# A two-block transformer kernel: both products of the squared-ReLU MLP by seven quadrant products each

## The chip, the cores and the metric

The kernel runs on one core of a Trainium2 chip. The metric is the device time of one execution in microseconds (us). Five engines work in parallel and meet at semaphores: PE (TensorE, matrix products), ACT (ScalarE), DVE (VectorE), POOL (GpSimd) and SP (SyncE, which issues the DMAs here). Each engine runs its own queue in order.

## What is computed

The program is two transformer blocks over 1024 tokens of width 1024 in float32. The first block has retention, a gated delta rule and a mixture of experts, the second neighbourhood attention, gated linear attention and an MLP. The change lies in the MLP at the end of the second block:

```
def sqrelu_mlp(h, ln_g, w1, w2):           # h 1024x1024, w1 1024x4096, w2 4096x1024
    u = rmsnorm_2(h, ln_g) @ w1
    return jnp.square(jax.nn.relu(u)) @ w2

h = h + sqrelu_mlp(h, ...)
return rmsnorm_2(h, ln_final_g)
```

## The kernel before, in words

Every float32 product is made of three matmuls in the reduced format fp32r: an operand x is split into hi (ACT copies x to fp32r, which rounds it) and lo (DVE computes x minus hi), and a product is hi·hi + hi·lo + lo·hi (`mm3`, L637; `wsplit`, L622). Each matmul takes a 128x128 weight block and streams 512 columns into one of the eight banks of PSUM.

`mlp` (L2223) first normalises the eight token tiles of `xres` and transposes them on PE into hi and lo parts that stay in SBUF (`normed_T`, `to_T`). Then a loop over 16 slices of 256 hidden channels does both products in turn. For the first, `chan_block` (L679) makes four PSUM tiles of 128 channels by 512 tokens with 24 matmuls each, and `ev_u` (L2241) applies ReLU and square and splits the result. For the second, `wload` fetches two blocks of w2, and for each of 16 tiles 6 matmuls go to PSUM, which DVE adds to `xres` (L2256). A slice has 96 + 96 = 192 matmuls, the loop 3072. Weights come from DRAM in 512 KB loads; activations and `xres` stay in SBUF throughout. At the end each token tile is normalised once more and stored (L2258 to L2265).

The order of instructions is not that of the code. `Program.record` (L325) notes every operation with its dependences, `price` (L358) gives it a cost, and `flush` (L404) plays all engines forward and emits each queue in the order so found, with the longest remaining path first. In its model POOL and DVE do not slow each other; a 1024-element `tensor_tensor` costs 1.14 us on DVE and 2.21 us on POOL, a 512-column fp32r matmul 0.213 us. Since one function emits everything, nearly all rows of the profile show line 346. SBUF is divided by hand into a float32 and an fp32r area; `Pool.tile` gives out slots in rings, and a write into a slot waits for the last readers of what was there (`alloc`, L188).

Of the kernel before, what the change touches and what calls it, by code (L numbers as in the profile page):

```python
# [12 lines left out]
F32R = mybir.dt.float32r  # L13
I32 = mybir.dt.int32
BF = mybir.dt.bfloat16
AF = mybir.ActivationFunctionType
OP = mybir.AluOpType
# [4 lines left out]
T = 1024  # L22
D = 1024
NT = 8
# [22 lines left out]
LANES = 8  # L47
TABLES = {'Exp': (0,), 'Tanh': (0, 18), 'Silu': (18,), 'Sin': (9, 18), 'Ln': (5,)}
RMW = ('copy_predicated',)


class Op:
# [102 lines left out]
class Program:  # L155
# [169 lines left out]
    def record(self, eng, name, real, a, k):  # L325
# [10 lines left out]
        for key, v in list(enumerate(args)) + list(k.items()):  # L336
            if key == 'accum_out':
                writes.append(v)
            elif key != 'out':
                if isap(v):  # L340
                    reads.append(v)
                elif isinstance(v, bass.IndirectOffsetOnAxis):
                    reads.append(v.ap)
        if name in RMW or (name == 'matmul' and not k.get('start', True)):
            reads.append(out)
# [150 lines left out]
class Cols:  # L496
# [3 lines left out]
    def add(self, name, a):  # L500
        a = np.asarray(a, np.float64)
        if a.ndim == 1:
            a = np.broadcast_to(a[None, :], (128, a.shape[0]))
        a = a.reshape(128, -1)
        self.at[name] = (self.n, a.shape[1])
        self.parts.append(a.astype(np.float32))
        self.n += a.shape[1]
# [53 lines left out]
class Kern:  # L561
# [1276 lines left out]
    def mixer2(self):  # L1838
        nc, ins = self.nc, self.ins
        w_in = ins['w_in_2'][0]  # L1840
        self.banks = {'acc': (0, 1), 'tp': (2, 3), 'sm': (4, 5), 'ga': (6, 7)}
        c0 = ExitStack()
# [6 lines left out]
        h = self.new_hT(self.pool('h2', ctx=ch))  # L1849
# [24 lines left out]
        pa = self.pa = self.pool('pa', ctx=ca)  # L1874
# [25 lines left out]
        py = self.pool('y', ctx=self.cy)  # L1900
# [4 lines left out]
        with ca:  # L1905
            self.banks.update({'sc': (0, 2), 'tp': (4, 5), 'po': (6, 7)})
            cs = ExitStack()
            self.pst = self.pool('ns', ctx=cs)
            with ExitStack() as cf:
                pf = self.pool('pf', ctx=cf)  # L1910
                slots = [[(pf if i == 3 else self.pst).get(1024, f'n{i}{j}', F32R) for i in range(4)]
                         for j in range(2)]
            order = [slots[j][i] for i in range(3) for j in range(2)]
            for n, name in enumerate(('naq', 'nakh', 'nakl')):
                self.pst.tags[name] = ([order[n], order[n + 3]], [0])
            self.P = []
            for i in range(5):
                P = self.t(pa, [128, 640], tag=f'P{i}')
                nc.gpsimd.memset(P[:, 512:640], 0.0)
                self.P.append(P)  # L1920
            self.pn = 0
            for hp in range(4):
                self.prog.boost = 0. if hp < 1 else 0.0
                st = self.na_stack(hp)
                for i in range(2):
                    self.na_head(2 * hp + i, st[i])
            self.prog.boost = 0.0
            cs.close()
            for i in range(2):
                y[i].append(self.t(py, [128, 8, 4, 128], F32R, tag=f'y{i}1'))  # L1930
            for tt in range(NT):
                ts = slice(tt * 128, tt * 128 + 128)
                g = self.t(pa, [128, 512], tag='gg', bufs=1)
                s = self.t(pa, [128, 512], tag='gs', bufs=1)
                nc.sync.dma_start(g, self.gla_d[ts])
                nc.sync.dma_start(s, self.gs_d[ts])
                nc.gpsimd.tensor_tensor(out=g, in0=g, in1=s, op=OP.mult)
                self.to_T(g, [y[0][1][:, tt]], [y[1][1][:, tt]])
        self.banks = {'acc': (0, 1, 2, 3), 'tp': (4, 5), 'sm': (6, 7)}
        self.cxp = ExitStack()  # L1940
        xp = self.pool('x2', ctx=self.cxp)
# [3 lines left out]
        for cb in range(2):  # L1945
            cs = slice(512 * cb, 512 * cb + 512)
# [3 lines left out]
            self.tok_block(ins['w_out_2'][0], 512 * cb, y, ev_o)  # L1950
        for tt in range(NT):
            self.tap('hm', self.xres[tt], slice(tt * 128, tt * 128 + 128))
        c0.close()

    def normed_T(self, pn, x, row, h, tt):
        r = self.sumsq(pn, x, 'nt')
# [263 lines left out]
                                  sr.rearrange("p h e -> p (h e)"))  # L2220


    def mlp(self):  # L2223
        nc, ins = self.nc, self.ins
        V = nc.vector
        w1, w2 = ins['w_ff1_2'][0], ins['w_ff2_2'][0]
        h = self.y
        with ExitStack() as cn:
            pn = self.pool('pn2', ctx=cn)
            row = self.bcast_row(ins['ln_ff_g_2'][0], D, 'row', pn)  # L2230
            for tt in range(NT):
                self.normed_T(pn, self.xres[tt], row, h, tt)
        for tag in ('whi', 'wlo'):
            self.wp.trim(tag, 3)
        self.nw = 3
        with ExitStack() as cu:
            pu = self.pool('pu', ctx=cu)
            for e in range(16):
                uh, ul = [self.t(pu, [128, 2, T], F32R, tag=n) for n in ('uh', 'ul')]
                for m in range(2):  # L2240
                    def ev_u(half, tok, p):  # L2241
                        t = self.t(pu, [128, 512], tag='ut', bufs=2)
                        nc.scalar.activation(t, p, AF.Relu)
                        nc.scalar.activation(uh[:, m, tok], t, AF.Square)
                        V.tensor_tensor(out=t, in0=t, in1=t, op=OP.mult)
                        V.tensor_tensor(out=ul[:, m, tok], in0=t, in1=uh[:, m, tok], op=OP.subtract)
                    self.chan_block(w1, 256 * e + 128 * m, 128, h, ev_u)
                for cb in range(2):
                    cs = slice(512 * cb, 512 * cb + 512)
                    wh, wl = self.wload(w2, 256 * e, 512 * cb, 2, 512)  # L2250
                    for tt in range(NT):
                        ts = slice(tt * 128, tt * 128 + 128)
                        p = self.ps([128, 512], 'acc')
                        for k in range(2):
                            self.mm3(p, uh[:, k, ts], ul[:, k, ts], wh[:, k], wl[:, k], k == 0, k == 1)
                        V.tensor_tensor(out=self.xres[tt][:, cs], in0=self.xres[tt][:, cs], in1=p, op=OP.add)  # L2256
        self.cy.close()
        with ExitStack() as cf:  # L2258
            pf = self.pool('pf2', ctx=cf)
            row = self.bcast_row(ins['ln_final_g_2'], D, 'row', pf)  # L2260
            for tt in range(NT):
                xt = self.xres[tt]
                r = self.sumsq(pf, xt, 'fn')
                V.scalar_tensor_tensor(xt, xt, r, row, op0=OP.mult, op1=OP.mult)
                nc.sync.dma_start(self.out[tt * 128:(tt + 1) * 128], xt)  # L2265
        self.cxp.close()
# [20 lines left out]
```

## Time and profile before

| | us |
|---|---|
| three runs | 2833.72 (median), 2832.54, 2833.97 |
| the profiled execution, its own time | 2830.14 |
| its span, first to last instruction | 2828.1 |
| first matmul of the MLP loop starts | 2114.37 |
| granted clock of TensorE, mean | 0.983 of 2.4 GHz |

The span starts with the first instruction; all positions below are us from there. A row of the timeline merges neighbouring instructions of one kind (x4 is four of them) and gives the start of the first and the time from there to the end of the last. A duration includes time in which an instruction that has been started is held up. The spacing of starts tells what one costs in a full queue.

### The profile page before, as it was taken

The numbers are of one execution on the slowest core, as the hardware profiler recorded it, in microseconds if no ns is written. First come the engines' busy times: TensorE is split into PE (matmuls) and PEld (weight loads), VectorE is DVE, ScalarE is ACT, GpSimd is POOL, SyncE is SP. The second block draws the span as 40 slices with busy tenths as digits, with TensorE's granted clock in tenths as the row PEclk, the third lists the DMA queues.
The fourth block names the chain that finished last, engine by engine and source line by source line (L and its number), as shares of the span: only waits on it lengthen the run. The fifth ranks groups of instructions, "written<-read, shape, count | busy, mean of one in ns | idle before, by whom it ended". The sixth has DMA issues, their size and how long they took to land. (4 is left out here: it accounts for less than half of the span.)

```text
span 2828.1 us, 36441 instructions
## 1 busy us (share of the span) xinstructions
PE 2663.9 (94%) x13174; PEld 2048.9 (72%) x13174; DVE 1705.0 (60%) x2575; ACT 1117.4 (40%) x1960; POOL 622.5 (22%) x675
## 2 busy tenths in 40 slices
PE   5999999999978999999986999999999999999998
PEld 4787788997757776454435777777888888888886
DVE  7557676555679888786766335277445454444445
ACT  4333223333136677565545434357422212122122
POOL 2106433432442111322136012144110000000001
PEclk9999999999979999999998999999999999999999
DMA  9443246246348999999978343263211111111111
GB/s 243 91 138 88 93 149 165 80 157 230 143 165 287 344 349 341 352 323 361 341 245 295 121 125 110 72 172 94 94 42 52 38 52 52 45 52 53 45 53 67
DMA packets 305621, 446.82 MB, mean 158 GB/s; under 512 B 61274, under 2 KB 135694, under 8 KB 304414
## 3 DMA queue, kind: packets, MB, share of 16 engines
q1 hardware_dynamic: 298782, 427.68, 46.5%
q0 software_dynamic: 6656, 16.79, 1.7%
q8 instruction: 105, 1.72, 0.2%
q14 instruction: 78, 0.64, 0.1%
HBM read 384.54 MB, written 65.75 MB: 159 GB/s over the span
## 5 line engine op out<-in xcount | busy, mean ns | idle before, releaser
L346 PE MATMUL psum_all<-sbuf 128*128 128x512 f32 (+10 forms) x13174 | 2663.9, 363 | 151.7 <-DVE sbuf L346 99.9
L346 PEld LDWEIGHTS psum_all<-sbuf 128*128 128x128 f32 (+7 forms) x13174 | 2048.9, 176 | 766.3 <-issue 167.3
L346 ACT ACTIVATE sbuf<-sbuf 128x1024 fp32r<-128x1024 f32 (+9 forms) x792 | 707.6, 914 | 781.3 <-PE psum_all L346 536.3
L346 DVE TENSOR_TENSOR sbuf<-sbuf,sbuf 128x1024 fp32r<-128x1024 f32 (+3 forms) x538 | 616.8, 1166 | 277.6 <-ACT sbuf L346 269.0
L346 ACT ACTIVATE sbuf<-psum_all 128x512 f32<-128x512 f32 (+14 forms) x798 | 377.9, 485 | 886.1 <-PE psum_all L346 839.7
L346 POOL TENSOR_TENSOR sbuf<-sbuf 128x512 f32<-128x512 f32 (+7 forms) x325 | 384.3, 1190 | 576.7 <-DVE sbuf L346 474.4
L346 DVE TENSOR_TENSOR sbuf<-sbuf,psum_all 128x512 f32<-128x512 f32 (+4 forms) x359 | 239.1, 673 | 165.2 <-PE psum_all L346 164.6
L346 DVE TENSOR_TENSOR sbuf<-sbuf 128x512 f32<-128x512 f32 (+9 forms) x285 | 205.2, 734 | 203.6 <-ACT sbuf L346 175.5
L346 POOL TENSOR_SCALAR sbuf<-sbuf 128x1 f32<-128x1 f32 (+3 forms) x182 | 75.3, 415 | 994.9 <-ACT sbuf L346 902.7
L346 DVE TENSOR_TENSOR sbuf<-psum_all,sbuf 128x512 fp32r<-128x512 f32 (+13 forms) x306 | 182.3, 607 | 158.0 <-ACT sbuf L346 78.1
L346 DVE SCALAR_TENSOR_TENSOR sbuf<-sbuf 128x512 f32<-128x512 f32 (+5 forms) x247 | 196.3, 801 | 55.6 <-POOL sbuf L346 43.1
L346 DVE TENSOR_SCALAR sbuf<-sbuf 128x32 f32<-128x32 f32 (+7 forms) x220 | 111.2, 518 | 48.1 <-ACT sbuf L346 22.7
L1728 POOL DMA_INDIRECT y_d<-sbuf x35 | 57.4, 1641 | 195.8 <-DVE sbuf L346 194.5
L346 DVE SCALAR_TENSOR_TENSOR sbuf<-psum_all,sbuf 128x128 f32<-128x128 f32 (+9 forms) x109 | 62.0, 585 | 40.0 <-PE psum_all L346 39.5
L1716 POOL DMA_INDIRECT sbuf<-h_d,sbuf x35 | 45.1, 1288 | 186.2 <-PE psum_all L346 153.2
L346 DVE SCALAR_TENSOR_TENSOR sbuf<-sbuf,psum_all 128x128 f32<-128x128 f32 (+1 forms) x100 | 38.2, 409 | 76.7 <-PE psum_all L346 51.8
L346 DVE CUSTOM_DVE_ANT_0 sbuf<-psum_all,sbuf 128x512 f32<-128x512 f32 (+2 forms) x80 | 48.1, 613 | 24.8 <-PE psum_all L346 24.2
L346 DVE COPY sbuf<-psum_all 128x512 f32<-128x512 f32 (+9 forms) x55 | 31.7, 576 | 39.9 <-PE psum_all L346 39.7
L346 POOL MEMSET sbuf<- 64x64 f32 (+10 forms) x54 | 16.8, 313 | 174.4 <-DVE sbuf L346 91.9
L346 POOL TENSOR_TENSOR sbuf<-sbuf,sbuf 128x1024 fp32r<-128x1024 f32 x16 | 40.1, 2510 | 61.7 <-ACT sbuf L346 48.4
L346 ACT ACTIVATE sbuf<-psum_all,sbuf 128x128 f32<-128x128 f32 (+1 forms) x72 | 24.4, 405 | 23.4 <-PE psum_all L346 17.7
L346 ACT ACTIVATION_READ_ACCUMULATOR sbuf<-sbuf 128x1 f32 x152 | 28.9, 190 | 0.0
(18 smaller groups left out, 111.8 us busy)
## 6 DMA issues: line engine op xcount, KB each, us to landing
sbuf<-in_w SPq DMA_DIRECT2D x384, 512.0 KB
sbuf<-in_w_ff SPq DMA_DIRECT2D x64, 512.0 KB
sbuf<-in_w_in SPq DMA_DIRECT2D x56, 512.0 KB
sbuf<-in_w_ada SPq DMA_DIRECT2D x48, 512.0 KB
sbuf<-in_x SPq DMA_DIRECT2D x16, 512.0 KB
sbuf<-in_w_out SPq DMA_DIRECT2D x16, 512.0 KB
sbuf<-y_d SPq DMA_DIRECT2D x8, 1024.0 KB
qkv_d<-sbuf SPq DMA_DIRECT2D x12, 512.0 KB
```

The lines of the kernel that those rows point to most:

```text
L346: op = self.new_op(eng, lambda: real(*a, **k), name, reads, writes)
L1716: return self.prog.real.gpsimd.indirect_dma_start(out=xg, out_offset=None, in_=self.h2_d, in_offset=bass.IndirectOffsetOnAxis(ap=tok, axis=0),
L1728: st = self.prog.real.gpsimd.indirect_dma_start(out=self.y_d, out_offset=bass.IndirectOffsetOnAxis(ap=dest, axis=0), in_=y, in_offset=None ...
```

## The change

`mlp` is rewritten. The two products (1024x1024 by 1024x4096, and 1024x4096 by 4096x1024) become eight products of 1024x1024 by 1024x1024, four for each. Each of these is cut into 512x512 quadrants and made by `wino` with seven quadrant products in place of eight (the Winograd form of Strassen's algorithm). The sums and differences of quadrants are made in place by `both`, on POOL (`G`) for six quadrants and on DVE (`V`) for two. Each quadrant product splits both its operands (four calls of `split`, each an ACT copy and a DVE subtraction of 1024 elements per partition) and runs 48 matmuls into four PSUM banks; two such sets of four take turns. `ev_u` and `ev_y` combine the results: in the first phase into tiles `s1` and `s7` in SBUF and squared-ReLU outputs, which go to DRAM (`u_d`), in the second into `xres`. Quadrants are loaded from DRAM for each group, activations too; the normalised input goes to `h_d` and `xres` to `x_d` and back. The weight buffers `wraw` go, and `whi` and `wlo` get 13 slots each. The final norm is as before, on a fresh `xres`.

```
@@ mixer2 @@
                 self.to_T(g, [y[0][1][:, tt]], [y[1][1][:, tt]])
+        c0.close()
         self.banks = {'acc': (0, 1, 2, 3), 'tp': (4, 5), 'sm': (6, 7)}
...
-        c0.close()
@@ new functions, and mlp @@
+    def wino(self, q, evac):
+        nc = self.nc
+        def split(x):
+            hi = self.t(self.wp, [128, 2, 512], F32R, tag='whi', bufs=self.nw)
+            lo = self.t(self.wp, [128, 2, 512], F32R, tag='wlo', bufs=self.nw)
+            nc.scalar.activation(hi, x, AF.Copy)
+            nc.vector.tensor_tensor(out=lo, in0=x, in1=hi, op=OP.subtract)
+            return hi, lo
+        def prod(n, a, b):
+            ops = []
+            for j in range(2):
+                s = slice(2 * j, 2 * j + 2)
+                ops.append((split(q[a][:, s]), split(q[b][:, s])))
+            self.nprod += 1
+            ps = [self.prog.psum_tile([128, 512], 'wino', (4 * (self.nprod % 2) + t,)) for t in range(4)]
+            first = None
+            for j, ((ah, al), (bh, bl)) in enumerate(ops):
+                for t, p in enumerate(ps):
+                    m = slice(128 * t, 128 * t + 128)
+                    for k in range(2):
+                        for i, (x, y) in enumerate(((ah, bh), (ah, bl), (al, bh))):
+                            op = nc.tensor.matmul(p, x[:, k, m], y[:, k], start=j + k + i == 0, stop=j + k + i == 4)
+                            first = first or op
+                            op.head = first
+            for t, p in enumerate(ps):
+                evac(n, t, p)
+        def both(eng, out, a, b, op):
+            for j in range(2):
+                s = slice(2 * j, 2 * j + 2)
+                eng.tensor_tensor(out=q[out][:, s], in0=q[a][:, s], in1=q[b][:, s], op=op)
+        G, V = nc.gpsimd, nc.vector
+        prod(1, 'a11', 'b11')
+        prod(2, 'a12', 'b21')
+        both(G, 'a21', 'a11', 'a21', OP.subtract)
+        both(V, 'b12', 'b22', 'b12', OP.subtract)
+        prod(7, 'a21', 'b12')
+        both(G, 'a21', 'a22', 'a21', OP.subtract)
+        both(V, 'b12', 'b11', 'b12', OP.add)
+        prod(6, 'a21', 'b12')
+        both(G, 'a11', 'a21', 'a11', OP.add)
+        both(G, 'b11', 'b22', 'b12', OP.subtract)
+        prod(5, 'a11', 'b11')
+        both(G, 'a12', 'a12', 'a21', OP.subtract)
+        prod(3, 'a12', 'b22')
+        both(G, 'b21', 'b21', 'b12', OP.subtract)
+        prod(4, 'a22', 'b21')
+    def quad_load(self, q, name, part):
+        for j in range(2):
+            s = slice(2 * j, 2 * j + 2)
+            self.nc.sync.dma_start(q[name][:, s], part(j))
     def mlp(self):
         nc, ins = self.nc, self.ins
         V = nc.vector
         w1, w2 = ins['w_ff1_2'][0], ins['w_ff2_2'][0]
-        h = self.y
+        self.nprod = 0
+        x_d = self.dt([T, D], 'x_d')
+        h_d = self.dt([4 * 128, 2048], 'h_d')
+        u_d = self.dt([16 * 128, 2048], 'u_d')
+        cq = ExitStack()
+        pq = self.pool('qb', ctx=cq)
+        q = {n: self.t(pq, [128, 4, 512], tag=n) for n in ('b11', 'b21', 'b12', 'b22', 'a12')}
         with ExitStack() as cn:
             pn = self.pool('pn2', ctx=cn)
             row = self.bcast_row(ins['ln_ff_g_2'][0], D, 'row', pn)
             for tt in range(NT):
-                self.normed_T(pn, self.xres[tt], row, h, tt)
+                x = self.xres[tt]
+                r = self.sumsq(pn, x, 'nt')
+                t = self.t(pn, [128, D], tag='nh', bufs=2)
+                V.scalar_tensor_tensor(t, x, r, row, op0=OP.mult, op1=OP.mult)
+                for k in range(2):
+                    p = self.ps([128, 4, 128], 'tp')
+                    for i in range(4):
+                        nc.tensor.transpose(p[:, i, :], t[:, 512 * k + 128 * i:512 * k + 128 * i + 128], self.ident)
+                    b = q[f'b{k + 1}{tt // 4 + 1}'][:, :, 128 * (tt % 4):128 * (tt % 4) + 128]
+                    if k:
+                        V.tensor_copy(b, p)
+                    else:
+                        nc.scalar.activation(b, p, AF.Copy)
+                if tt % 4 == 3:
+                    for k in range(2):
+                        i = 2 * k + tt // 4
+                        b = q[f'b{k + 1}{tt // 4 + 1}'].rearrange("p k n -> p (k n)")
+                        nc.sync.dma_start(h_d[128 * i:128 * i + 128], b)
+                nc.sync.dma_start(x_d[tt * 128:tt * 128 + 128], x)
+        self.cy.close()
+        self.wp.trim('wraw', 0)
+        pa = self.pool('qa', ctx=cq)
+        q.update({n: self.t(pa, [128, 4, 512], tag=n) for n in ('a11', 'a21', 'a22')})
+        self.cxp.close()
         for tag in ('whi', 'wlo'):
-            self.wp.trim(tag, 3)
-        self.nw = 3
+            self.wp.reserve(tag, 1024, 8, F32R)
+        self.nw = 13
         with ExitStack() as cu:
             pu = self.pool('pu', ctx=cu)
-            for e in range(16):
-                uh, ul = [self.t(pu, [128, 2, T], F32R, tag=n) for n in ('uh', 'ul')]
-                for m in range(2):
-                    def ev_u(half, tok, p):
-                        t = self.t(pu, [128, 512], tag='ut', bufs=2)
-                        nc.scalar.activation(t, p, AF.Relu)
-                        nc.scalar.activation(uh[:, m, tok], t, AF.Square)
-                        V.tensor_tensor(out=t, in0=t, in1=t, op=OP.mult)
-                        V.tensor_tensor(out=ul[:, m, tok], in0=t, in1=uh[:, m, tok], op=OP.subtract)
-                    self.chan_block(w1, 256 * e + 128 * m, 128, h, ev_u)
-                for cb in range(2):
-                    cs = slice(512 * cb, 512 * cb + 512)
-                    wh, wl = self.wload(w2, 256 * e, 512 * cb, 2, 512)
-                    for tt in range(NT):
-                        ts = slice(tt * 128, tt * 128 + 128)
-                        p = self.ps([128, 512], 'acc')
-                        for k in range(2):
-                            self.mm3(p, uh[:, k, ts], ul[:, k, ts], wh[:, k], wl[:, k], k == 0, k == 1)
-                        V.tensor_tensor(out=self.xres[tt][:, cs], in0=self.xres[tt][:, cs], in1=p, op=OP.add)
-        self.cy.close()
+            for g in range(4):
+                for i, k in ((0, 0), (0, 1), (1, 0), (1, 1)):
+                    c = 1024 * g + 512 * i
+                    self.quad_load(q, f'a{i + 1}{k + 1}', lambda j: w1[
+                        512 * k + 256 * j:512 * k + 256 * j + 256, c:c + 512].rearrange("(a p) n -> p a n", p=128))
+                if g:
+                    for k, i in ((0, 0), (1, 0), (0, 1), (1, 1)):
+                        n = 2 * k + i
+                        self.quad_load(q, f'b{k + 1}{i + 1}', lambda j: h_d[
+                            128 * n:128 * n + 128, 1024 * j:1024 * j + 1024].rearrange("p (a n) -> p a n", a=2))
+                keep = {}
+                def new(n, t):
+                    r = keep[n, t] = self.t(pu, [128, 512], tag=f's{n}', bufs=4)
+                    return r
+                def out(i, j, t, a, b):
+                    u = self.t(pu, [128, 512], tag='u', bufs=5)
+                    V.tensor_tensor(out=u, in0=a, in1=b, op=OP.add)
+                    V.scalar_tensor_tensor(u, u, 0.0, u, op0=OP.max, op1=OP.mult)
+                    n = 4 * g + 2 * i + j
+                    nc.sync.dma_start(u_d[128 * n:128 * n + 128, 512 * t:512 * t + 512], u)
+                def ev_u(n, t, p):
+                    if n in (1, 7):
+                        nc.scalar.activation(new(n, t), p, AF.Copy)
+                        return
+                    u, v = keep[1, t], keep.get((7, t))
+                    if n == 2:
+                        out(0, 0, t, u, p)
+                    elif n == 6:
+                        V.tensor_tensor(out=u, in0=u, in1=p, op=OP.add)
+                        nc.gpsimd.tensor_tensor(out=v, in0=u, in1=v, op=OP.add)
+                    elif n == 5:
+                        out(1, 1, t, v, p)
+                        V.tensor_tensor(out=u, in0=u, in1=p, op=OP.add)
+                    elif n == 3:
+                        out(0, 1, t, u, p)
+                    else:
+                        out(1, 0, t, v, p)
+                self.wino(q, ev_u)
+        self.cxp = ExitStack()
+        xp = self.pool('x3', ctx=self.cxp)
+        xres = [self.t(xp, [128, D], tag=f'x{tt}') for tt in range(NT)]
+        for tt in range(NT):
+            nc.sync.dma_start(xres[tt], x_d[tt * 128:(tt + 1) * 128])
+        py = self.pool('y3', ctx=cq)
+        for g in range(4):
+            for i, k in ((0, 0), (0, 1), (1, 0), (1, 1)):
+                n = 4 * g + 2 * k + i
+                self.quad_load(q, f'a{i + 1}{k + 1}', lambda j: u_d[
+                    128 * n:128 * n + 128, 1024 * j:1024 * j + 1024].rearrange("p (a n) -> p a n", a=2))
+            for k, i in ((0, 0), (1, 0), (0, 1), (1, 1)):
+                c = 1024 * g + 512 * k
+                self.quad_load(q, f'b{k + 1}{i + 1}', lambda j: w2[
+                    c + 256 * j:c + 256 * j + 256, 512 * i:512 * i + 512].rearrange("(a p) n -> p a n", p=128))
+            def ev_y(n, t, p):
+                here, there = {1: ('00 01', '10 11'), 2: ('00', ''), 7: ('10 11', ''), 6: ('01', '10 11'),
+                               5: ('01 11', ''), 3: ('01', ''), 4: ('10', '')}[n]
+                def add(eng, names, src):
+                    for i, j in names.split():
+                        x = xres[4 * int(i) + t][:, 512 * int(j):512 * int(j) + 512]
+                        eng.tensor_tensor(out=x, in0=x, in1=src, op=OP.add)
+                add(V, here, p)
+                if there:
+                    s = self.t(py, [128, 512], tag='s', bufs=2)
+                    nc.scalar.activation(s, p, AF.Copy)
+                    add(nc.gpsimd, there, s)
+            self.wino(q, ev_y)
+        cq.close()
         with ExitStack() as cf:
             pf = self.pool('pf2', ctx=cf)
             row = self.bcast_row(ins['ln_final_g_2'], D, 'row', pf)
             for tt in range(NT):
-                xt = self.xres[tt]
+                xt = xres[tt]
                 r = self.sumsq(pf, xt, 'fn')
                 V.scalar_tensor_tensor(xt, xt, r, row, op0=OP.mult, op1=OP.mult)
                 nc.sync.dma_start(self.out[tt * 128:(tt + 1) * 128], xt)
```

## Rows read from the trace of the kernel before

**Rows 1.** The page's first part: busy time of each engine, its share of the span, and its instructions.
```profile
PE 2663.9 (94%) x13174; PEld 2048.9 (72%) x13174; DVE 1705.0 (60%) x2575; ACT 1117.4 (40%) x1960; POOL 622.5 (22%) x675
```

**Rows 2.** Busy time by stretch, here the MLP loop: bounds of the stretch, its length, then busy us and instructions of each engine, granted clock (1.00 is 2.4 GHz), DMA share and GB/s.
```profile
core 0: us, PE busy (x) PEld busy (x) DVE busy (x) ACT busy (x) POOL busy (x), PEclk, DMA share, GB/s
...
2108.00:2815.00 707.00, 705.67 (x3134) 583.98 (x3133) 341.09 (x469) 156.03 (x218) 5.83 (x13) 1.00 0.15 49
```

**Rows 3.** The chain of waits that ended last, in order of time: start, us, what.
```profile
2115.19 693.63 PE psum_all L346 x3076
...
2821.48 1.28 DVE sbuf L346
```

**Rows 4.** Groups of instructions by shape in the MLP loop, 2108 to 2815: busy us, mean ns of one, then idle time of the engine before them.
```profile
L346 PE MATMUL psum_all<-sbuf 128*128 128x512 f32 x3090 | 703.0, 389 | 1.2 <-ACT sbuf L346 1.2
...
L346 DVE TENSOR_TENSOR sbuf<-sbuf,psum_all 128x512 f32<-128x512 f32 x255 | 171.7, 683 | 80.7 <-PE psum_all L346 80.7
L346 DVE TENSOR_TENSOR sbuf<-sbuf,sbuf 128x1024 fp32r<-128x1024 f32 x64 | 78.3, 1223 | 140.5 <-ACT sbuf L346 140.4
L346 ACT ACTIVATE sbuf<-sbuf 128x1024 fp32r<-128x1024 f32 x64 | 67.9, 1061 | 356.6 <-PE psum_all L346 356.0
...
L346 ACT ACTIVATE sbuf<-psum_all 128x512 f32<-128x512 f32 x64 | 37.6, 588 | 174.0 <-PE psum_all L346 173.9
```

**Rows 5.** Timeline of ACT, 2400 to 2450: the same weight split in two successive slices of the loop.
```profile
2401.97 1.06 ACT L346 ACTIVATE sbuf<-sbuf 128x1024 fp32r<-128x1024 f32 x1 [3.95 <-PE psum_all L346]
...
2445.49 1.06 ACT L346 ACTIVATE sbuf<-sbuf 128x1024 fp32r<-128x1024 f32 x1 [3.95 <-PE psum_all L346]
```

**Rows 6.** Timeline of DVE in the MLP loop, queue full: PSUM reads and SBUF operations of 512 elements in turn.
```profile
2404.21 0.68 DVE L346 TENSOR_TENSOR sbuf<-sbuf,psum_all 128x512 f32<-128x512 f32 x1
2404.81 0.68 DVE L346 TENSOR_TENSOR sbuf<-sbuf 128x512 f32<-128x512 f32 x1
2405.41 0.68 DVE L346 TENSOR_TENSOR sbuf<-sbuf,psum_all 128x512 f32<-128x512 f32 x1
2406.01 0.69 DVE L346 TENSOR_TENSOR sbuf<-sbuf,sbuf 128x512 fp32r<-128x512 f32 x1
```

**Rows 7.** Timeline of DVE in the mixture of experts, 1140 to 1156: weight splits with PSUM reads between them.
```profile
1144.85 4.61 DVE L346 TENSOR_TENSOR sbuf<-sbuf,sbuf 128x1024 fp32r<-128x1024 f32 x4
1149.38 0.41 DVE L346 TENSOR_TENSOR sbuf<-psum_all,sbuf 128x256 fp32r<-128x256 f32 x1
1149.72 2.34 DVE L346 TENSOR_TENSOR sbuf<-sbuf,sbuf 128x1024 fp32r<-128x1024 f32 x2
1151.99 1.39 DVE L346 SCALAR_TENSOR_TENSOR sbuf<-psum_all,sbuf 80x512 f32<-80x512 f32 x2
```

**Rows 8.** Timeline of POOL over the same time.
```profile
1145.16 8.06 POOL L346 TENSOR_TENSOR sbuf<-sbuf 64x512 f32<-64x512 f32 x1 [4.01 <-DVE sbuf L346]
...
1156.92 1.27 POOL L346 TENSOR_TENSOR sbuf<-sbuf 64x512 f32<-64x512 f32 x1 [2.44 <-DVE sbuf L346]
```

**Rows 9.** Timeline of DVE, then of POOL, at 708 to 712: a 1024-element POOL operation behind a DVE operation on SBUF.
```profile
708.51 1.22 DVE L346 TENSOR_TENSOR sbuf<-sbuf 128x1024 f32<-128x1024 f32 x1
709.75 0.26 DVE L346 SCALAR_TENSOR_TENSOR sbuf<-psum_all,sbuf 128x36 f32<-128x36 f32 x1
...
708.67 3.32 POOL L346 TENSOR_TENSOR sbuf<-sbuf 128x1024 f32<-128x1024 f32 x1 [1.40 <-DVE sbuf L346]
```

**Rows 10.** Timeline of POOL, then of DVE, at 850 to 862: the other way round.
```profile
850.41 2.40 POOL L346 TENSOR_TENSOR sbuf<-sbuf,sbuf 128x1024 fp32r<-128x1024 f32 x1 [4.56 <-ACT sbuf L346]
...
855.92 5.09 POOL L346 TENSOR_TENSOR sbuf<-sbuf,sbuf 128x1024 fp32r<-128x1024 f32 x2 [0.27 <-DMA sbuf<-in_w]
...
858.69 3.41 DVE L346 TENSOR_TENSOR sbuf<-sbuf,sbuf 128x1024 fp32r<-128x1024 f32 x1
```

**Rows 11.** Timeline of POOL, then of DVE, at 722 to 724: DVE reads PSUM while POOL works.
```profile
722.43 1.29 POOL L346 TENSOR_TENSOR sbuf<-sbuf 128x512 f32<-128x512 f32 x1 [5.24 <-DVE sbuf L346]
...
722.72 1.29 DVE L346 TENSOR_TENSOR sbuf<-psum_all,sbuf 128x512 fp32r<-128x512 f32 x2 [0.37 <-ACT sbuf L346]
```

**Rows 12.** Timeline of PE at the start of the MLP (512-column matmuls; transposes lie between the two rows).
```profile
2094.83 18.29 PE L346 MATMUL psum_all<-sbuf 128*128 128x512 f32 x92
2114.37 1.85 PE L346 MATMUL psum_all<-sbuf 128*128 128x512 f32 x8 [1.25 <-ACT sbuf L346]
```

**Rows 13.** Timeline of PE at the end of the MLP.
```profile
2794.82 20.79 PE L346 MATMUL psum_all<-sbuf 128*128 128x512 f32 x91
```

**Rows 14.** Busy time by stretch in the mixture of experts, where PE has to wait; columns as in the second group.
```profile
800.00:1000.00 200.00, 172.40 (x796) 135.43 (x795) 175.45 (x312) 113.88 (x140) 57.42 (x45) 0.91 0.81 291
1400.00:1600.00 200.00, 168.25 (x713) 104.25 (x712) 122.23 (x129) 103.57 (x148) 69.04 (x71) 0.95 0.69 241
```

**Rows 15.** The page's second part: what the DMA engines moved in each fortieth of the span.
```profile
GB/s 243 91 138 88 93 149 165 80 157 230 143 165 287 344 349 341 352 323 361 341 245 295 121 125 110 72 172 94 94 42 52 38 52 52 45 52 53 45 53 67
```

More of the change, by code (lines that the diff above doesn't have):

```diff
@@ L49 @@
 RMW = ('copy_predicated',)
+QUADS = ('a11', 'a12', 'a21', 'a22', 'b11', 'b12', 'b21', 'b22')
 class Op:
```

## The prediction

> **What bounds the kernel now.** The page's first part has PE busy for 94% of the span and no other engine above 60% [rows 1]. That is an average, so the next view is the busy time by stretch: in the MLP loop PE works 705.67 of 707 us at full clock, with DVE at 48%, ACT at 22% and POOL at 1% [rows 2]. The chain of waits says the same in one row: 693.63 us of PE matmuls, and no wait in between [rows 3]. So before the change nothing but the number of matmuls counts in this stage. Their price is the pace of the loop, not the mean duration of 389 ns [rows 4], in which neighbours overlap: the same weight split returns after 2445.49 - 2401.97 = 43.52 us [rows 5], a slice has 192 matmuls, so one costs 226.7 ns. The loop is 16 x 43.52 = 696.3 us.
>
> **PE's part.** The change leaves 8 x 7 x 48 = 2688 matmuls of the same shape, each with its own weight load as before: 2688 x 226.7 ns = 609.3 us, or 10.88 us for a quadrant product and 76.2 us for a group of seven. That is 87.0 us less, and the most that can be had.
>
> **What it adds on DVE and POOL, in three kinds.** The new question is whether the other engines keep up with 76.2 us for a group. The three kinds of operation behave differently.
>
> S: DVE operations with both inputs in SBUF. 28 splits and 4 additions of 1024 elements in a group; four in a row take 4.61 us, the last alone 1.2, so one costs 1.13 us in a full queue [rows 7]. In the first phase also 16 squared-ReLUs of 512 elements, at the 0.60 us between starts of such operations [rows 6]. First phase 32 x 1.13 + 16 x 0.60 = 45.8 us, second 36.2 us.
>
> P: DVE operations that read PSUM, also 0.60 us [rows 6]. First phase 24 (14.4 us), second 40 (24.0 us).
>
> G: POOL additions. 12 of 1024 elements in a group, and 4 (first phase) or 16 (second) of 512.
>
> DVE alone needs 60 us in either phase and POOL 32 to 46. If they ran beside each other, PE would set the pace. The rows say that S and G do not. A POOL operation started at 1145.16 took 8.06 us instead of the 1.27 of its sister [rows 8], while DVE ran splits [rows 7]; it ended 1.16 us after the last of them. At 708.67 one of 1024 elements ended 2.26 us after DVE's SBUF operation did [rows 9]. The other way round, a split that started at 858.69 while POOL worked took 3.41 us and ended 1.09 us after POOL [rows 10]. P is free of it: two PSUM reads beside a POOL operation took 1.29 us together, and POOL its plain 1.29 [rows 11]. So S and G share one resource, and their sum is a floor for a group: first phase 45.8 + 12 x 2.26 + 4 x 1.16 = 77.5 us, second 36.2 + 12 x 2.26 + 16 x 1.16 = 81.9 us. Both lie above PE's 76.2. P comes on top unless G runs during it: with every P beside G the eight groups take 4 x (77.5 + 81.9) = 637.6 us, with none 637.6 + 4 x (14.4 + 24.0) = 791.2 us. The old loop, 696.3, lies in between.
>
> Where in between? POOL got in when DVE turned to PSUM or stopped, not between two splits [rows 7, 8]. A POOL addition that starts at a PSUM read covers at least this read. The first phase has 16 G for 24 P, in the second 28 G for 40 P, of which many come in pairs (products 1, 5 and 7 add each bank twice). I take 70% of P covered in the first and 80% in the second phase: 81.8 and 86.7 us a group, 674.0 us in all, 22.3 us less than now.
>
> The row on which the choice rests is weighed against the Trainium skill, page "SBUF — State Buffer", section "Who interferes with whom": DVE and POOL share a port pair as an exclusive lock, and the one that issues first has it for the whole instruction. That the lock exists, the rows agree. By its order POOL's operation at 1145.16 would have gone after the one split then in flight; the row shows five more ahead of it. By that order POOL's additions would stand between splits, where they cover no PSUM read, and the sum would go towards the 791.2.
>
> **What else it adds.** ACT: 28 copies of 1024 at 1.06 us and 8 PSUM copies at 0.59 [rows 4] are 34 us of a group; hidden by PE, and in the second phase ACT can stop behind the two slots of tile `s`, which wait for POOL (with the splits queued behind it; part of the slower rival). Loads and stores: 8 MB in and, in the first phase, 4 MB out for a group, some 150 GB/s against the 340 that the mixture of experts sustains [rows 15]; 32 issues on SP in 82 us. Hidden by the quadrant products ahead: a first-needed quadrant such as a11 has its last split for product 5, two products before the group ends. If the cover goes, a boundary costs a product (rival three).
>
> Start of the MLP: the first product needs all of b11, then one more ACT copy and DVE subtraction (1.06 + 1.22 us [rows 4]) that the old loop did tile by tile, beside a DVE full of norms. Bounds 2.3 us and one product, 10.9; I take 5, nearer the lower, since a11 can be loaded and split before. Today 1.2 us of wait shows there [rows 12]. Storing `h_d` and `x_d` is hidden by these products. Change of phase: `xres` comes back from DRAM into memory that the first phase has just left; the first read is due after one product (10.9 us), so nothing; with the cover gone 0 to 10.9. End: the last matmul ends at 2815.6 [rows 13], the last norm at 2822.8 [rows 3]; the same chain after, for four late tiles instead of eight: nothing, within 3 us either way.
>
> Clock: where PE waits, the granted clock falls. Busy 86% of 200 us it was granted 0.91, busy 84% in another stretch 0.95 [rows 14]. PE would now need 76.2 of some 84 us. At 0.95 that is 80 us, still inside; at 0.91 it is 84, all of it. I take 1 us a group, 8 us; bounds 0 and 25.
>
> **Sum.** -22.3 + 5 + 8 = -9.3 us. The profiled execution took 2830.14 us (span 2828.1), 3.6 below the median; the difference carries over, so 2833.7 - 9.3 = 2824.4 us. Its own range is 2800 to 2842: from 85% of P covered without a clock loss to 65% with 18 us of it.
>
> **Rivals.** First, PE stays the bound: additions on POOL fall where DVE waits for PE, so that S and G together fit, against the floor by only 1 to 6 us a group. 609.3 + 5 instead of 696.3: 2752 us. For it: DVE waited for PE for 81 us of the old loop [rows 4], and these waits are open to POOL. Against: 77.5 and 81.9 are above 76.2 before anything is late.
>
> Second, the slower one: POOL's additions find no cover. A sum of quadrants lies in a chain (split 7, subtract, split 6, add, split 5), and POOL starves behind a run of splits as at 1145.16 [rows 8]; DVE then runs out of work, and the PSUM reads have been made alone. With half of P covered: 714.4 + 13 - 696.3 = +31 us, 2865 us; with none, 2942 us. It decides from 30% of P uncovered, (696.3 - 13 - 637.6) / 153.6. My estimate has 24% uncovered, so there is little room. By the Trainium skill's order of issue, cited above, this is the likelier case; the row speaks against that order, so it has no more than its share of this rival's chance.
>
> Third, loads come late: each quadrant has one buffer and SP's queue is in order, so loads of the next group can stand behind a store that waits for a result. One product lost at each of 7 boundaries is 76 us: 2901 us. Against it: products 5, 3 and 4, some 33 us of PE work, lie between the last use of a11 and its next.
>
> That the change doesn't save the matmuls can be ruled out: they are counted in the code.
>
> **Chances.** Forecast 0.47, PE bound 0.18, uncovered 0.27, late loads 0.08. A measurement of this kernel tells 0.2%, 5.7 us, from no change. Of the forecast's own range, 0.30 lies below 2828, 0.11 within 5.7 us, 0.06 above. Faster 0.30 + 0.18 = 0.48, same 0.11, slower 0.06 + 0.27 + 0.08 = 0.41: the sign is nearly open. Range: from the PE bound, 2752, up past the half-covered case with the larger clock loss (2865 + 17 and the start's bound), 2890; about 2 in 10 lie outside.
>
> **What would show it.** Right: PE's share of the MLP falls from 100% to about 90%, with matmuls waiting for DVE and ACT; POOL's 1024-element additions last well over 2.4 us on average and DVE's splits well over 1.22; DVE is busy nearly throughout; the granted clock falls below 1 in places. The steps: some 82 us between like products of successive groups in the first phase, 87 in the second. Wrong: PE at full share and groups of 76 us (first rival); groups over 90 us with POOL operations of 5 us and more (second); PE waiting for DMA at the start of groups (third). Splits and POOL additions that overlap at their plain durations would overturn the argument.

## The result, and the profile after

| | before | after |
|---|---|---|
| median of the runs, us | 2833.13 | 2860.96 (2857.63 to 2862.97) |
| span of the profiled execution, us | 2828.1 | 2860.3 |
| first matmul of the loop to end of the last, us | 2114.37 to 2815.61 = 701.2 | 2122.07 to 2848.43 = 726.4 |
| mean granted clock | 0.983 | 0.968 |

The ratio is 1.0098, 95% interval 1.008 to 1.0115: the changed kernel is 28 us slower. The spans differ by 32.2 us; 7.7 of them lie ahead of the first quadrant product, 25.1 in the loop, and the end is 0.6 us shorter.

The page's first part of the changed kernel, beside [rows 1]:
```profile
PE 2619.6 (92%) x12790; PEld 1997.9 (70%) x12790; DVE 2070.4 (72%) x2695; ACT 1229.0 (43%) x2048; POOL 1089.6 (38%) x851
```
384 matmuls are gone, as counted. But DVE is busy 365 us longer and POOL 467. By stretch, the two phases of the loop (columns as in [rows 2], where the old loop had PE at full share and clock):
```profile
2122.00:2484.00 362.00, 326.77 (x1357) 262.75 (x1358) 345.01 (x285) 136.18 (x154) 191.28 (x68) 0.94 0.44 151
2484.00:2848.00 364.00, 325.62 (x1349) 263.78 (x1349) 355.46 (x298) 123.00 (x146) 280.71 (x121) 0.94 0.27 93
```
The bound has moved: DVE is at 95% and 98%, PE at 90% with a lower clock. What PE waits for in the loop (engine waited for, us, times, longest):
```profile
PE psum_all L347 <- DVE sbuf L347: 70.7, 25, 9.3
PE psum_all L347 <- ACT sbuf L347: 2.8, 3, 1.5
```
The groups of instructions by shape in the loop, 2122 to 2848, beside [rows 4]:
```profile
L347 DVE TENSOR_TENSOR sbuf<-sbuf,sbuf 128x1024 fp32r<-128x1024 f32 x220 | 416.3, 1931 | 1.3 <-issue 1.2
L347 POOL TENSOR_TENSOR sbuf<-sbuf 128x1024 f32<-128x1024 f32 x96 | 306.2, 3212 | 188.3 <-DVE sbuf L347 104.7 <-issue 42.3 <-DMA sbuf<-in_w_ff 31.1
...
L347 DVE TENSOR_TENSOR sbuf<-sbuf,psum_all 128x512 f32<-128x512 f32 x255 | 160.6, 674 | 5.8 <-PE psum_all L347 5.0 <-ACT sbuf L347 0.7
L347 POOL TENSOR_TENSOR sbuf<-sbuf 128x512 f32<-128x512 f32 x80 | 158.7, 2012 | 54.0 <-ACT sbuf L347 35.0 <-DVE sbuf L347 18.8
```
What counts here is the mean of one. A split lasts 1.93 us instead of 1.22. POOL's additions last 3.21 and 2.01 us, where a POOL operation of the same size took 2.40 [rows 10] and 1.29 [rows 11] before. A PSUM read lasts 0.674, against 0.683 before. Only what shares the resource has become longer. One stretch of the second phase in the timeline, POOL and then DVE:
```profile
2534.42 10.04 POOL L347 TENSOR_TENSOR sbuf<-sbuf 128x1024 f32<-128x1024 f32 x3
...
2533.83 8.39 DVE L347 TENSOR_TENSOR sbuf<-sbuf,sbuf 128x1024 fp32r<-128x1024 f32 x3
```
Three POOL additions in 10.04 us are 3.35 us each, the 2.26 us of one plus the 1.09 that a split needs after it [rows 9, 10]: here they take turns, one for one. Of the 96 additions of this size in the loop 62 last 3.2 to 3.5 us, as in such a turn; 31 last less than 3 us and three last 5.1, 7.7 and 8.1.

### The profile page after: what moved, and what is told of

Its sections match the earlier page's. It is cut to its first block, busy times and chain, and to the rows that moved or that the text cites. A ratio compares the mean times of both kernels' runs of the same rounds, so it can differ in the third digit from the quotient of the medians.

```text
span 2860.3 us, 36673 instructions
## 1 busy us (share of the span) xinstructions
PE 2619.6 (92%) x12790; PEld 1997.9 (70%) x12790; DVE 2070.4 (72%) x2695; ACT 1229.0 (43%) x2048; POOL 1089.6 (38%) x851
## 5 line engine op out<-in xcount | busy, mean ns | idle before, releaser
L347 PE MATMUL psum_all<-sbuf 128*128 128x512 f32 (+9 forms) x12790 | 2619.6, 366 | 228.8 <-DVE sbuf L347 172.5
L347 PEld LDWEIGHTS psum_all<-sbuf 128*128 128x128 f32 (+6 forms) x12790 | 1997.9, 177 | 850.1 <-issue 206.1
L347 POOL TENSOR_TENSOR sbuf<-sbuf 128x512 f32<-128x512 f32 (+7 forms) x501 | 848.3, 1709 | 832.4 <-DVE sbuf L347 609.7
L347 ACT ACTIVATE sbuf<-sbuf 128x1024 fp32r<-128x1024 f32 (+9 forms) x888 | 826.7, 959 | 784.5 <-PE psum_all L347 320.0
L347 DVE TENSOR_TENSOR sbuf<-sbuf,sbuf 128x1024 fp32r<-128x1024 f32 (+1 forms) x634 | 916.1, 1475 | 138.2 <-ACT sbuf L347 128.7
L347 DVE SCALAR_TENSOR_TENSOR sbuf<-sbuf 128x512 f32<-128x512 f32 (+5 forms) x311 | 267.8, 871 | 55.7 <-POOL sbuf L347 45.2
L347 DVE TENSOR_TENSOR sbuf<-sbuf,psum_all 128x512 f32<-128x512 f32 (+4 forms) x359 | 228.0, 667 | 93.6 <-PE psum_all L347 92.2
L347 DVE TENSOR_TENSOR sbuf<-psum_all,sbuf 128x512 f32<-128x512 f32 (+13 forms) x290 | 171.8, 603 | 156.2 <-ACT sbuf L347 74.1
L347 DVE TENSOR_TENSOR sbuf<-sbuf 128x1024 f32<-128x1024 f32 (+6 forms) x253 | 223.4, 899 | 83.1 <-ACT sbuf L347 38.3
```

Source lines behind the costliest of these rows:

```text
L347: op = self.new_op(eng, lambda: real(*a, **k), name, reads, writes)
```

## The experiments

Theory: POOL additions and DVE operations with both inputs in SBUF exclude each other, and their sum, with the PSUM reads that nothing covers, sets the pace. Rivals: DVE is overloaded and slow by itself; the chain of quadrant sums is too long in latency; loads come late. Times are medians; the kernel before stood at 2833 to 2834 us beside all of these.

**All quadrant sums on DVE** (`e1_sums_dve`).
```
-        G, V = nc.gpsimd, nc.vector
+        G, V = nc.vector, nc.vector
```


> All quadrant sums on DVE, none on POOL. Exclusion theory (POOL additions and DVE operations with both inputs in SBUF never run together): a group then has 13.6 us more of DVE's SBUF work and 27.1 us less of POOL's, 64 us and 68 us of both in the two phases, with 14.4 and 24 us of PSUM reads beside or after them; PE's 76 us sets the pace again. MLP loop 615 to 640 us, total 2750 to 2785. Rival, DVE is simply overloaded and its splits are slow for another reason: 96 more operations of 1.13 us or more on the busiest engine, total 2960 or more. Rival, the chain of sums is too long in latency: a sum falls from 3.2 to about 1.2 us, faster too, about 2780; this run does not tell it from the first.

Measured: 2780.2 us, ratio to before 0.9811 (0.9795 to 0.9828); faster than both kernels, with 96 operations more on the engine that was the bound. The total is inside what the first theory expected; the loop, 640.2 us from its first matmul (2125.89 to 2766.05), is at the upper end of its range. The loop's stretches, first and second phase:
```profile
2122.00:2437.00 315.00, 311.78 (x1386) 256.81 (x1384) 311.89 (x343) 141.14 (x157) 29.23 (x18) 1.00 0.54 184
2437.00:2766.00 329.00, 309.79 (x1337) 251.58 (x1337) 321.98 (x340) 127.33 (x147) 165.49 (x75) 0.99 0.28 96
```
In the first phase PE is back at 99% and full clock. The overload rival is out.

**POOL only writes** (`e2_pool_memset`).
```
+                if eng is nc.gpsimd:
+                    eng.memset(q[out][:, s], 0.5)
+                    eng.memset(q[out][:, s], 0.25)
+                else:
...
```


> Leaves out the quadrant sums on POOL: in the place of each half of a sum POOL writes the same tile twice with a constant, so the chain of dependences and the queues stay, but POOL reads nothing. Exclusion theory, if it is POOL's reading that excludes: two writes of 0.95 us instead of 2.26, DVE's splits fall from 1.92 to near 1.22 us, PE sets the pace, total about 2765. If POOL's writing excludes as well: splits about 1.8 us, total 2830 or more. Rival, DVE overloaded by itself: 2861, splits still 1.9 us.

Measured: 2750.3 us (ratio 0.9704, 0.9684 to 0.9723), 15 us under the total expected. Two splits that overlap POOL's four writes in the timeline, and the writes:
```profile
2295.74 1.22 DVE L347 TENSOR_TENSOR sbuf<-sbuf,sbuf 128x1024 fp32r<-128x1024 f32 x1 [0.21 <-ACT sbuf L347]
2296.51 3.88 POOL L347 MEMSET sbuf<- 128x1024 f32 x4 [6.89 <-DMA sbuf<-in_w_ff]
2299.78 1.23 DVE L347 TENSOR_TENSOR sbuf<-sbuf,sbuf 128x1024 fp32r<-128x1024 f32 x1 [2.82 <-ACT sbuf L347]
```
Both engines keep their plain durations, so POOL's reading excludes, its writing not. The two rows are no exception: in the loop 83 splits have nothing but such writes beside them, with a mean of 1.22 us and none over 1.23. All 220 splits together have a mean of 1.38 us, not 1.22, because POOL's 80 additions of 512 elements still read. After the first 16 matmuls of the loop PE runs through:
```profile
2129.81 609.62 PE L347 MATMUL psum_all<-sbuf 128*128 128x128 f32 x2690 [0.75 <-DVE sbuf L347]
```
That is close to PE's floor, 609.3 us by the prediction; from its first matmul the loop takes 613.0 us (2126.44 to 2739.43).

**POOL repeats the sums for nobody** (`e3_pool_repeats`): all sums on DVE, and in the first phase the same sums on POOL into a tile that is not read.
```
+                if eng is nc.gpsimd and self.junk is not None:
+                    eng.tensor_tensor(out=self.junk, in0=q[a][:, s], in1=q[b][:, s], op=op)
+                nc.vector.tensor_tensor(out=q[out][:, s], in0=q[a][:, s], in1=q[b][:, s], op=op)
...
```


> All quadrant sums on DVE, and in the first phase POOL makes the same sums once more into a tile that nobody reads, so nothing waits for POOL's result. Exclusion theory: in the first phase 59.4 + 31.7 = 91 us of excluded work in a group and about half of 14.4 us of PSUM reads uncovered, 98 us; second phase as with all sums on DVE, about 79; loop about 708 us, total 2843, 60 to 90 us over the kernel with all sums on DVE. Rival, the latency of the chain: POOL is out of the chain, so the time is that of the kernel with all sums on DVE, within 10 us.

Measured: 2866.5 us, 86 more than with all sums on DVE. That is inside the 60 to 90 that the first theory expected, though 23 us above its total. The stretches show it in the first phase alone, 397 us against 315; the second has 330 against 329. (All stretches start at 2122; the loop's first matmul starts at 2118.33 here and at 2125.89 with all sums on DVE, so from there it is 401 us against 311.)
```profile
2122.00:2519.00 397.00, 321.16 (x1314) 258.17 (x1313) 387.70 (x329) 132.12 (x147) 174.32 (x64) 0.88 0.41 136
2519.00:2849.00 330.00, 317.68 (x1377) 259.24 (x1376) 322.95 (x347) 128.34 (x146) 161.56 (x74) 0.99 0.30 100
```
Four squared ReLUs on DVE in this phase, held up and not:
```profile
2245.09 10.58 DVE L347 SCALAR_TENSOR_TENSOR sbuf<-sbuf 128x512 f32<-128x512 f32 x4
...
2263.66 2.48 DVE L347 SCALAR_TENSOR_TENSOR sbuf<-sbuf 128x512 f32<-128x512 f32 x4
```
POOL is not wholly out of the chain. The sums are made in place, so DVE may write a half only after POOL has read it. DVE's sums up to 2520 us:
```profile
L347 DVE TENSOR_TENSOR sbuf<-sbuf 128x1024 f32<-128x1024 f32 x67 | 107.4, 1622 | 5.9 <-POOL sbuf L347 4.6 <-ACT sbuf L347 1.2
```
They waited 4.6 us for POOL, and DVE was busy in 387.7 of the 397 us. So nearly all of the difference lies in operations that last longer beside POOL's work, whose result nobody uses; latency in the chain does not carry the loss.

**All eight sums on POOL** (`e4_sums_pool`).
```
-        G, V = nc.gpsimd, nc.vector
+        G, V = nc.gpsimd, nc.gpsimd
```


> The two sums that DVE made go to POOL as well. Exclusion theory: 4.5 us of DVE's SBUF work in a group become 9.0 us on POOL, 4.5 us more of the sum, 36 us in all: total about 2897, 2880 to 2915. Rival, DVE overloaded: 36 us less, 2825.

Measured: 2861.9 us, no different from the change. Neither expectation holds. Its loop takes 726.7 us (2122.36 to 2849.05); the excluded work is up by 36 us to 673.8, and what the loop has above it is down by as much, from 88.8 to 52.9 us. My expectation held the covered share fixed. Counted from the starts and ends of the instructions in the two traces, PSUM reads with no POOL addition beside them take 43.0 us instead of the change's 68.8, and both engines are idle for 3.3 us instead of 11.8: the more POOL had to do, the more PSUM reads fell beside it.

**Sums on DVE in the first phase only** (`e5_sums_dve_first`).
```
+        G, V = nc.vector if self.first else nc.gpsimd, nc.vector
...
```


> All quadrant sums on DVE in the first phase, as in the change (six of eight on POOL) in the second. Exclusion theory: the phases are separate stages, so the first takes what it takes with all sums on DVE (about 311 us) and the second what it takes in the change (about 364): total about 2780 + 35 = 2815, 2805 to 2825. If one phase held all of the loss, 2780 or 2861.

Measured: 2815.6 us. The phases add up: 315 us to 2437 as with all sums on DVE, 364 us after it as in the change.

**POOL out of the loop** (`e6_no_pool`): besides, DVE makes the addition of product 6 in the first phase and all additions from PSUM in the second.
```
-                        nc.gpsimd.tensor_tensor(out=v, in0=u, in1=v, op=OP.add)
+                        V.tensor_tensor(out=v, in0=u, in1=v, op=OP.add)
...
-                if there:
-                    ...
+                add(V, there, p)
```


> All sums on DVE, and POOL out of the loop altogether: in the first phase DVE makes the addition for product 6, in the second it adds every product to its tiles straight from PSUM. Exclusion theory: nothing holds DVE up, so its operations last their plain 1.21 and 0.67 us and a group takes DVE's own sum where that is over PE's 76.2: first phase 45.8 + 13.6 + 2.4 + 14.4 = 76.2, second 49.8 + 56 x 0.60 = 83.4 us. Loop 640 to 655 us, total 2775 to 2795, about that of all sums on DVE, although DVE makes 96 operations more. Rival, DVE overloaded: those 96 operations come on top, 2780 + 58 = 2838.

Measured: 2786.9 us (0.9848, 0.983 to 0.9866). Nothing on DVE is longer than its plain duration:
```profile
L347 DVE TENSOR_TENSOR sbuf<-sbuf,sbuf 128x1024 fp32r<-128x1024 f32 x220 | 258.1, 1212 | 0.0
...
L347 DVE TENSOR_TENSOR sbuf<-sbuf,psum_all 128x512 f32<-128x512 f32 x319 | 197.3, 674 | 6.7 <-PE psum_all L347 6.6
L347 DVE TENSOR_TENSOR sbuf<-sbuf 128x1024 f32<-128x1024 f32 x128 | 152.3, 1212 | 0.2 <-DMA sbuf<-in_w_ff 0.2
L347 DVE SCALAR_TENSOR_TENSOR sbuf<-sbuf 128x512 f32<-128x512 f32 x64 | 41.5, 679 | 0.0
```
The total is inside what was expected, 7 us over that with all sums on DVE. The second phase has 329 us, 82 a group, where the sum gave 83.4.

**Product 6 from PSUM by DVE in the second phase** (`e7_six_dve`), on top of all sums on DVE.
```
-                here, there = {... 6: ('01', '10 11'), ...}[n]
+                here, there = {... 6: ('01 10 11', ''), ...}[n]
```


> All sums on DVE, and in the second phase product 6 is added from PSUM by DVE alone; POOL keeps its eight additions for product 1. Exclusion theory: 9.3 us less on POOL, 4.8 us more of PSUM reads in a group; 49.8 + 9.3 + 28.8 = 87.9 us without any cover, some 83 with half of POOL's work beside the reads: total within 10 us of 2780.

Measured: 2779.3 us (0.9814, 0.9796 to 0.9832), no different from `e1_sums_dve`. What POOL gives up here, DVE takes over.

**Another price for the planner** (`e8_price`), on top of all sums on DVE.
```
+                            op.cost = 226.7
```


> All sums on DVE, and the planner that orders the queues prices a matmul of the quadrant products at 226.7 ns instead of 213. Exclusion theory: the engines' work is the same, only the order can change, by which PE waits now some 23 us in the second phase; 2765 to 2785. No rival differs here; it asks whether the order is worth something.

Measured: 2793.2 us, 13 us over the same work in the other order, and outside what I expected. PE waits 29.5 us in the loop instead of 22.1. The order is worth this much; why the truer price gives the worse order stays open.

## Why the prediction was wrong

The forecast, 2824.4 us, had the wrong sign; the measured 2861 lies where the second rival put it, 2865 with half of the PSUM reads uncovered. That rival's mechanism came true in part: reads made alone, and a DVE that at times had no work. But its POOL operations of 5 us and more are only three of 96. Its 8 us for the clock stand where the trace has idle time of both engines and a larger S + G, so that its total came this close is in part luck.

Right were the steps up to the bounds. PE's floor of 609.3 us is close to what PE took once nothing held it up (609.62). That S and G exclude each other is shown by the splits' duration, which follows POOL's reading: 1931 ns in the change, 2070 with all sums on POOL, 1311 with all on DVE, 1212 with POOL idle, and plain beside POOL's writes. In the change the 88 splits with no POOL addition beside them last at most 1.23 us. The loop, 726.4 us, lies between the bounds of 637.6 and 791.2. Loads, the change of phase and the end are as priced, with one exception below; the start cost 7.7 us against 5.

The step that failed is the share of PSUM reads that POOL's work covers. I took 70% and 80%, which left 36 us of reads uncovered, 24% of them. The trace gives the share, counted from the starts and ends of both engines' instructions (POOL's are rough). In the first phase POOL worked during 16.1 of 52.6 us of reads, 31%; in the second during 62.4 of 94.7 us, 66%. So 68.8 us of reads had nothing beside them, 47%, where by the prediction 30% decides the sign. The rest of the loop's 726.0 us are 645.4 in which S or G ran, 8 us over their sum, and 11.8 in which neither engine worked, which I had at nothing. (DVE alone was idle for 726.0 - 700.5 = 25.5 us; in 13.7 of these POOL worked.)

Two readings led there. First, I concluded from POOL's 8.06 us [rows 7, 8] that POOL gets in at a PSUM read only. The row does not say so: at 1149.38 DVE read PSUM, and the two splits behind this read took their plain 2.34 us, so POOL did not get in there either. In the change POOL and DVE mostly take turns between splits, as the rows at 2534 show; the Trainium skill, "SBUF — State Buffer", "Who interferes with whom", has it so: the one that issues first goes first. Not always, though. Here POOL's first addition waits through a whole run of splits and squared ReLUs and takes 8.1 us, POOL and then DVE:
```profile
2443.68 10.49 POOL L347 TENSOR_TENSOR sbuf<-sbuf 128x1024 f32<-128x1024 f32 x2 [9.70 <-DMA sbuf<-u_d]
...
2443.13 2.35 DVE L347 TENSOR_TENSOR sbuf<-sbuf,sbuf 128x1024 fp32r<-128x1024 f32 x2
2445.40 1.88 DVE L347 SCALAR_TENSOR_TENSOR sbuf<-sbuf 128x512 f32<-128x512 f32 x3
2447.20 2.35 DVE L347 TENSOR_TENSOR sbuf<-sbuf,sbuf 128x1024 fp32r<-128x1024 f32 x2
```
I had weighed the rule and given one old row more weight. Had I followed it, the sum would have gone towards 791.2, too far the other way, but with the right sign. Second, I spread POOL's work over the group. It comes in runs, when a quadrant's inputs are there: POOL's 1024-element additions had 188 us of idle time before them in the loop, 105 of it for DVE. While it ran it stood against splits, and reads that came at other times had no company. That the runs are the reason is inferred from the timeline; no run here spread POOL's work.

Of DVE's idle 25.5 us, 16.6 come before its own first-phase subtractions, which wait for a group's quadrants (the third rival's mechanism, at a fifth of its price):
```profile
L347 DVE TENSOR_TENSOR sbuf<-sbuf 128x1024 f32<-128x1024 f32 x18 | 29.5, 1648 | 16.6 <-DMA sbuf<-h_d 10.7 <-DMA sbuf<-in_w_ff 5.9
```
With all sums on DVE this wait is 1.3 us in the whole loop.

The 8 us for the clock cannot be found apart. The clock did fall, to 0.94 in the loop and 0.88 in the first phase of `e3_pool_repeats`, where PE waited. But PE was not the bound there, and DVE, which was, waited only 5.0 us for PE before its PSUM reads. So the slower PE seems to have filled time that it would have waited; no run separates this.

## What to carry to other kernels

Before work moves to POOL to relieve DVE, add up what the two do on SBUF with two inputs: the sum counts, and an addition that takes 1.13 us on DVE and 2.26 on POOL makes it larger. The arithmetic saved on PE was real, but 87 us of matmuls were paid for with some 310 us of POOL work, which the planner's model counts as parallel to DVE's. With the sums left on DVE the same change gains 54 us. When a bound rests on how much is covered, and the sign hangs on that share, the share has to be worked out from when the covering work is ready, not from its amount.

## What the runs showed of the hardware

A POOL instruction that only writes does not hold up a DVE operation with two SBUF inputs: the splits beside such writes alone lasted 1.22 us on average in `e2_pool_memset`. Where both engines read SBUF for a while, they often take turns, one addition to one split, 3.35 us a pair. But a POOL addition can also wait through a run of DVE operations, as in the old row [rows 7, 8] and in the change at 2443.68 us. What decides between the two stays open.
